# Six weight blocks with stored low parts, and a reordered end, in a one-core hybrid decoder step

## The chip, the cores and the metric

The kernel runs on one core of a Trainium2 chip. The time is device microseconds of one execution; the figure compared is the median over runs. A core has TensorE (PE, matmul), VectorE (DVE), ScalarE (ACT), GpSimd (POOL) and SyncE (SP), which here only issues DMAs; 16 DMA engines carry the transfers that SP and POOL issue.

## The reference, cut to what matters

One step of a two-layer decoder over 1024 prompt tokens and 8 decode tokens, model width 2048, all in f32. Layer 0 is a pooling mixer, layer 1 attention with a window of 128. Both have an input projection to 4096 channels, a gate, an output projection and a LayerNorm over the residual. The change lies in the second layer's output projection and the norm behind it:

```python
    y = (o * jax.nn.silu(gate)) @ w_out
    return layer_norm(ALPHA * x + y, g_ln, b_ln)
```

with

```python
    mu = jnp.mean(xf, axis=-1, keepdims=True)
    var = jnp.mean(jnp.square(xf - mu), axis=-1, keepdims=True)
    return ((xf - mu) * lax.rsqrt(var + LN_EPS) * g + b)
```

## The kernel before

**Two halves, ten phases.** The 1032 tokens are two halves of 512 and 520. `PHASES` runs the projections of the halves in turn; the last two are `bo`, the second layer's output projection, for half 0 and then half 1. Activations stand transposed, 128 channels on the partitions and tokens along the row.

**A product in three.** An f32 product is made of rounded f32r parts: a block of weights (128x1024) is cast to its high part (`cast_to`, ScalarE, L506), the low part is the difference (`prep_to`, VectorE, L521), and TensorE multiplies high by high, high by low and low by high (L687, L688, L689).

**Seven blocks for a pair.** Channels are done in pairs of 128 by a seven-product Strassen form (`seven`). A block is one of the seven, 24 products of 128x128 by half the tokens, named (p, i): pair p of eight, product i of seven. Some blocks are read from the input `wob`, others from sums formed earlier and stored (`swob`). `begin`, ahead of every block, keeps the stream running: it requests weights up to seven blocks ahead (`load_to`, SP's queue), casts up to four and subtracts up to three ahead. After a block its bank of sums is taken up by VectorE or ScalarE in the posts; with `split`, as in the last phase, products 5 and 6 are added on VectorE (L639, L658).

**Order.** Instructions of TensorE, VectorE and ScalarE run in the order of the source (`in_order`); SP's and POOL's are placed by a scheduler. Buffers are 54 slots of SBUF; `Mem.full` hands out the one that was released longest ago, and `free(stored=True)` makes a slot that a store still reads count as released later.

**The end of half 1** is written by hand in `phase_end`. Pairs 4 to 7, called w, x, y, z, run in the order `TAIL`, whose last eight blocks are (4, 5), (4, 6), (5, 5), (5, 6), (6, 5), (6, 6), (7, 5), (7, 6). The half's 520 tokens are cut in two: `Bh`, the second 260, is complete after (w, 5), and its LayerNorm (`stats`, then per pair `affine1` on VectorE, L1493 and L1497, and `affine2` on ScalarE, L1504, with a store) runs while TensorE does the last eight blocks. `A`, the first 260, is complete only after (7, 6). `steps` gives what is issued after each block: `rest` adds the residual, `square` squares (L1456), `add` adds a pair into the running sums av and qv (L1459, L1460), `scale` multiplies by the norm's gain (L1516), `spare` copies the last four tokens aside on POOL (L1519), `back` reloads a pair.

After the last block: `sums_a` multiplies the running sums with J, a matrix of 1/2048 (L1552), `sums_z` adds pair z (L1560): this gives mean and mean square. `turn` transposes the scaled pairs into token rows (L1607). `moments` works out the reciprocal root with a Newton step (L1575 to L1587) and splits the row factors into high and low (`back32`, L1572). `last_rows` adds them to the transposed rows as a product (L1615) with tiles of gain and bias, which `rows0`, `rows1` and `rows2` prepare through a small DRAM tile, `gbd` (twelve row loads, L1542). `evict` takes the rows out (VectorE L1627, ScalarE L1629) and stores them (L1631). `last_four` does the four tokens on POOL (L1639 to L1643).

Of the kernel before, what the change touches and what calls it, by code (L numbers as in the profile page):

```python
# [70 lines left out]
)  # L71

LATE = ()
FORM = (0, 1)
X_KEEP = 5
X_AGE = 3
# [23 lines left out]
class Slot:  # L100


    def __init__(self, mem, i, h, a):
        self.mem, self.i, self.h, self.a = mem, i, h, a

    @property
    def r(self):
# [6 lines left out]
        return self.r[:, : k * n].rearrange("p (k n) -> p k n", k=k)  # L114

    def free(self, stored=False):
        self.mem.release(self, 10 if stored else 0)


class View:  # L120
# [64 lines left out]
class Entry:  # L185


    def __init__(self, loads, make, src, after):
        self.loads, self.make, self.src, self.after = loads, make, src, after


class Kern:
    def __init__(self, ctx, tc, io):
        self.tc, self.io = tc, io
        self.nc = tc.nc
        pool = lambda name, **kw: ctx.enter_context(tc.tile_pool(name=name, **kw))
        one = pool("one", bufs=1)
        self.smp = pool("smp", bufs=2)
        dram = pool("dram", bufs=1, space=bass.MemoryType.DRAM)
        self.psd = [pool(f"psd{i}", bufs=1, space=bass.MemoryType.PSUM) for i in range(3)]  # L200
        self.pso = pool("pso", bufs=1, space=bass.MemoryType.PSUM)
        self.four = None
        ctx.callback(self.use_four, None)
        self.prm = one.tile([P, N_PRM], F32, name="prm")
        self.cst = one.tile([P, N_CST], F32, name="cst")
        self.mki = self.cst[:, K_MP : K_MP + P].bitcast(I32)
        self.jr = one.tile([P, P], F32R, name="jr")
        self.nsink = self.prm[:, C_SINK : C_SINK + NH]
        self.area = one.tile([P, 4 * 64 + 16], F32, name="area")
        cut = lambda a, k, n: self.area[:, a : a + k * n].rearrange("p (k n) -> p k n", k=k)  # L210
        self.carry = cut(0, NK, NST)
        self.qd = [cut(64 * i, NDEC, 8) for i in range(2)]
        self.sgd = [cut(64 * i + 128, 8, NDEC) for i in range(2)]
        self.kdec = cut(256, 2, NDEC)
        self.mem = Mem(pool("mem", bufs=1), NSLOT)
        self.n = 0
        self.i = self.e = self.lastO = self.turns = self.ring = 0
        self.posts, self.events, self.side = [], {}, []
        self.extra, self.on = None, False
        self.fresh = False  # L220
        self.ahead = 7, 4, 3
        dr = lambda n, s: dram.tile(s, F32, tag=n, name=n)
        self.flip = 0
        self.Td, self.act, self.l_sq, self.l_sh = {}, {}, {}, {}
        for c, (_, T) in enumerate(CHUNKS):
            for n, k in (("x", "ai"), ("g", "ao"), ("h", "bi"), ("o", "bo")):
                if (k, c) in STRASSEN:
                    self.Td[n, c] = dr(f"t{n}{c}", [P, 8, 4, T // 2])
            self.act["x", c] = io[f"x{c}"]
            for n in ("g", "h", "o", "p"):  # L230
                self.act[n, c] = dr(f"{n}{c}", [P, NK, T])
        self.gbd = dram.tile([32, 2 * P], F32, tag="gbd", name="gbd")
        self.rows = [dr(f"rows{i}", [2, 32 * TMAX]) for i in range(4)]
        self.turned = 0
        self.ws = {
            n: [dr(f"s{n}{q}", [P, 4, 1024]) for q in range(np_)]
            for n, np_ in (("wia", 16), ("woa", 8), ("wkv", 2), ("wib", 16), ("wob", 8))
        }
# [141 lines left out]
    def build_stream(self):  # L380
        io = self.io
        w = []
        for kind, c, part in PHASES:
# [18 lines left out]
            elif kind == "bi":  # L402
                if part[0] == 0:
                    w += self.next_pairs("wkv", range(2), locked) if seven else pr("wkv", 0) + pr("wkv", 1)
                if seven:
                    for p in range(*part):
                        for q in (p, 8 + p):
                            if c == 1 and p in FORM:
                                f = self.first_pair("wib", q, False)
                                w += [f[i] for i in ORDER7]  # L410
                            else:
                                w += pr("wib", q)
                else:
                    for p in range(*part):
                        q, g = ((self.bare_pair if p in FORM else pr)("wib", q) for q in (p, 8 + p))
                        w += q[:2] + g[:2] + q[2:] + g[2:]
            else:
                name = "woa" if kind == "ao" else "wob"
                if (kind, c, part) != PHASES[-1]:
                    prs = [self.next_pair(name, q) for q in range(8)]  # L420
                    if (kind, c) == ("bo", 0):
                        for q in LATE:
                            prs[q] = self.first_pair(name, q)
                    w += [pr[i] for i in ORDERL for pr in prs[:2]]
                    w += [pr[i] for pr in prs[2:] for i in ORDER7]
                    continue
                w += self.next_pairs(name, range(SPLIT[0]), locked)
                late = {q: self.next_pair(name, q) for q in SPLIT}
                w += [late[q][i] for q, i in TAIL]
        self.stream = w  # L430
        self.loaded = self.made = self.cast = self.prepped = 0
        self.hl, self.late = {}, []

    def sum_gen(self, name):

# [60 lines left out]
    def load_to(self, n):  # L496
        while self.loaded < min(n, len(self.stream)):
            for go in self.stream[self.loaded].loads:
                go()
            self.loaded += 1  # L500

    def cast_to(self, n):
# [13 lines left out]
    def prep_to(self, n):  # L516
        self.cast_to(n)
        while self.prepped < min(n, len(self.stream)):
            s = self.stream[self.prepped]
            hi, lo = self.hl[self.prepped], self.mem.full(1024)  # L520
            self.nc.vector.tensor_sub(lo.r[:, :1024], s.src().a[:, :1024], hi.a[:, :1024])  # L521
            self.hl[self.prepped] = (hi, lo)
            for go in s.after:
                go()
            self.prepped += 1
# [892 lines left out]
    def phase_end(self, c, xs, x_in, pre, acc, gc, bc, out):  # L1418
# [128 lines left out]
        def sums_a():  # L1547

            R[0] = self.psW(), self.psW()
            for ps, a in zip(R[0], (av, qv)):  # L1550
                for j in range(2):
                    nc.tensor.matmul(  # L1552
                        ps[:, :TH], J, a[:, j, A], start=j == 0, stop=False, skip_group_check=True,
                    )

        def sums_z(n):

            w = (tv(z)[:, :, A], qh(z, A))[n]
            for j in range(2):
                nc.tensor.matmul(  # L1560
                    R[0][n][:, :TH], J, w[:, j], start=False, stop=j == 1, skip_group_check=True,
                )

        def moments():

# [13 lines left out]
            nc.vector.scalar_tensor_tensor(v, vb[:, :TH], EPS, qq, op0=ALU.add, op1=ALU.subtract)  # L1579
            affine1a(z, Bh)  # L1580
            nc.scalar.activation(r, v, AF.Abs_reciprocal_sqrt)
            affine2(y, Bh)
            nc.vector.tensor_mul(qq, r, r)
            nc.vector.scalar_tensor_tensor(qq, qq, -0.5, v, op0=ALU.mult, op1=ALU.mult)
            nc.vector.scalar_tensor_tensor(r, qq, 1.5, r, op0=ALU.add, op1=ALU.mult)
            nc.vector.tensor_mul(X[lo], v[lo, A2], r[lo, A2])
            nc.scalar.copy(M[lo], X[lo])  # L1587
            affine1b(z, Bh)
            back32(32)
            back32(96)  # L1590

        def factors():

# [54 lines left out]
        for p in SPLIT:  # L1648
            box, z0, z1 = self.two(T)

            def open_(p=p, box=box, z0=z0):
# [17 lines left out]
            (y, 3): [lambda: rest(x, A), lambda: sh.free()],  # L1669
            (z, 2): [rows0],  # L1670
            (z, 1): [rows1],
            (y, 4): [rows2],
            (z, 3): [lambda: rest(y, Bh), lambda: square(y, Bh), lambda: back(1)],
            (z, 4): [
                lambda: add(y, Bh), lambda: rest(y, A), lambda: back(2), lambda: back(3),
                lambda: spare(0), lambda: scale(0),
            ],
            (w, 6): [lambda: stats(Bh), lambda: spare(1), lambda: scale(1)],
            (x, 5): [lambda: square(w, A), lambda: affine(0, Bh), lambda: spare(2), lambda: scale(2)],
            (x, 6): [lambda: add(w, A), lambda: spare(w), lambda: scale(w)],  # L1680
            (y, 5): [lambda: square(x, A), lambda: affine(w, Bh), lambda: spare(3), lambda: scale(3)],
            (y, 6): [lambda: add(x, A), lambda: affine(1, Bh), lambda: spare(x), lambda: scale(x)],
            (z, 5): [lambda: square(y, A), lambda: affine(2, Bh), lambda: affine1(x, Bh)],
            (z, 6): [
                lambda: square(z, A, 0), lambda: add(y, A), lambda: scale(z, (0,), True), lambda: scale(y),
                lambda: spare(y), lambda: affine1(3, Bh), lambda: affine2(x, Bh),
            ],
        }
        for p, idx in TAIL:
            for go in steps.get((p, idx), []):  # L1690
# [11 lines left out]
        sums_a()  # L1702
        square(z, A, 1)
        affine1(y, Bh)
        scale(z, (1,))
        spare(z)
        sums_z(0)
        sums_z(1)
        X[0, 0], X[0, 1] = self.psD(), self.psD()
        turn(0, 0, 8)  # L1710
        X[0, 2], X[0, 3] = self.psW(), self.psW()
        turn(0, 8, 16)
        moments()
        X[1, 0], X[1, 1] = self.psO(), self.psD()
        turn(1, 0, 8)
        X[1, 2] = self.psW()
        turn(1, 8, 12)
        box["c"] = self.psW()
        factors()
        factors2()  # L1720
        affine2(3, Bh)
        last_rows(0, range(4))
        last_rows(1, range(3))
        evict(0, 0, False)
# [788 lines left out]
```

## Time and profile before

| what | value |
|---|---|
| median of three runs | 2303.64 us |
| lowest and highest | 2302.32 and 2305.52 us |
| the profiled execution | 2304.49 us |
| its span | 2302.7 us |
| PE busy | 2281.3 us (99%) |
| DVE busy | 1907.4 us (83%) |
| ACT busy | 1387.1 us (60%) |
| DMA moved | 654.07 MB, mean 284 GB/s |

The span is from the first to the last instruction. A row of the timeline gives start, length, engine, line, operation, result and operands, and the number merged into it; brackets give the idle time before it and what ended it. Products on TensorE overlap, so a product of 0.28 us is followed by the next after 0.12.

### The profile page before, as it was taken

To read this page: it belongs to the slowest core of one execution; us is meant where nothing else is said; L and a number is where in the kernel's file an instruction comes from. 1 tells how busy PE (TensorE), PEld (TensorE's weight loads), DVE (VectorE), ACT (ScalarE), POOL (GpSimd) and SP (SyncE) were. 2 spreads that over 40 slices of the span, in tenths; PEclk is the share of its full clock that TensorE was granted. 3 is DMA by queue.
4 is the path that set the end of the run, shared out by engine and by line. 5 is a ranking of instruction groups with operands and counts; after the bars stand their busy time and mean duration, and the time that the engine had idled before them with its cause. 6 is when DMAs were issued, how large, how long until landed. Compare 5 with 4: busy or idle time off the path is not lost. (4 is left out here: it accounts for less than half of the span.)

```text
span 2302.7 us, 50591 instructions
## 1 busy us (share of the span) xinstructions
PE 2281.3 (99%) x20353; PEld 2211.2 (96%) x20353; DVE 1907.4 (83%) x2429; ACT 1387.1 (60%) x2551; POOL 218.8 (10%) x399
## 2 busy tenths in 40 slices
PE   9999999999999999999999999999999999999998
PEld 8999999999999999999879999999999999999998
DVE  8888889877878898998868888899876777878997
ACT  5544446544546546655566667785766768656665
POOL 0111110011010010000111111101111010000001
PEclk9999999999999999999999999999999999999999
DMA  7869679988989999999677666777786878699894
GB/s 260 284 246 313 229 253 326 320 302 294 304 316 306 346 352 369 331 379 365 206 268 240 235 223 230 284 271 263 260 274 218 274 258 300 237 327 332 284 330 151
DMA packets 256956, 654.07 MB, mean 284 GB/s; under 512 B 27824, under 2 KB 116944, under 8 KB 256720
## 3 DMA queue, kind: packets, MB, share of 16 engines
q1 hardware_dynamic: 213568, 496.49, 63.7%
q0 software_dynamic: 43152, 154.34, 17.4%
q8 instruction: 159, 2.61, 0.5%
q14 instruction: 77, 0.63, 0.1%
HBM read 473.50 MB, written 177.23 MB: 283 GB/s over the span
## 5 line engine op out<-in xcount | busy, mean ns | idle before, releaser
L687 PE MATMUL pD<-m,m 128*128 128x260 f32 (+1 forms) x5088 | 1442.2, 283 | 3.9 <-ACT pD L626 2.2
L689 PE MATMUL pD<-m,m 128*128 128x260 f32 (+1 forms) x5088 | 1435.3, 282 | 6.1 <-DVE m L521 6.0
L688 PE MATMUL pD<-m,m 128*128 128x260 f32 (+1 forms) x5088 | 1435.0, 282 | 0.0
L687 PEld LDWEIGHTS pD<-m,m 128*128 128x128 f32 x5088 | 959.3, 189 | 13.1 <-issue 7.2
L689 PEld LDWEIGHTS pD<-m,m 128*128 128x128 f32 x5088 | 959.9, 189 | 8.6 <-DVE m L521 8.6
L688 PEld LDWEIGHTS pD<-m,m 128*128 128x128 f32 x5088 | 959.4, 189 | 0.5
L521 DVE TENSOR_TENSOR m<-m,m 128x1024 fp32r<-128x1024 f32 x690 | 832.6, 1217 | 85.7 <-ACT m L506 35.9
L506 ACT CAST m<-m 128x1024 fp32r<-128x1024 f32 x690 | 720.2, 1049 | 231.2 <-DVE m L352 98.8
L352 DVE TENSOR_TENSOR m<-m,m 128x1024 f32<-128x1024 f32 x128 | 156.4, 1222 | 12.2 <-DMA m<-in_wia 6.3
L850 DVE TENSOR_TENSOR m<-m,m 128x1024 fp32r<-128x1024 f32 (+1 forms) x118 | 143.9, 1225 | 3.9 <-ACT m L841 3.0
L841 ACT CAST m<-m 128x1024 fp32r<-128x1024 f32 (+1 forms) x118 | 123.4, 1053 | 3.7 <-DMA m<-in_x 2.4
L648 DVE TENSOR_TENSOR m<-pD,m 128x260 f32<-128x260 f32 (+1 forms) x92 | 39.0, 424 | 100.8 <-ACT pD L647 94.7
L660 ACT COPY m<-pD 128x260 f32<-128x260 f32 (+1 forms) x88 | 32.8, 372 | 122.5 <-PE pD L689 122.1
L1938 ACT ACTIVATE m<-m,sm 128x128 f32<-128x128 f32 x256 | 99.3, 391 | 0.0
L1187 PE MATMUL pD<-m,m 128*128 128x260 f32 (+1 forms) x528 | 91.5, 324 | 0.0
L635 ACT COPY m<-pD 128x260 f32<-128x260 f32 (+1 forms) x92 | 34.4, 373 | 93.1 <-PE pD L689 93.0
L715 PE MATMUL pD<-m,m 128*128 128x512 f32 x224 | 89.1, 398 | 0.0
L717 PE MATMUL pD<-m,m 128*128 128x512 f32 x224 | 88.4, 395 | 0.0
L716 PE MATMUL pD<-m,m 128*128 128x512 f32 x224 | 88.2, 394 | 0.0
L1187 PEld LDWEIGHTS pD<-m,m 128*128 128x128 f32 x528 | 79.4, 188 | 8.2
L632 ACT COPY m<-pD 128x260 f32<-128x260 f32 (+1 forms) x90 | 33.6, 373 | 87.4 <-PE pD L689 86.2
L626 ACT ACTIVATE pD<-pD 128x260 f32<-128x260 f32 (+1 forms) x90 | 33.2, 369 | 83.9 <-PE pD L689 83.4
(258 smaller groups left out, 2142.4 us busy)
## 6 DMA issues: line engine op xcount, KB each, us to landing
m<-in_wib SPq DMA_DIRECT2D x132, 512.0 KB
m<-in_wia SPq DMA_DIRECT2D x128, 512.0 KB
m<-swoa SPq DMA_DIRECT2D x64, 512.0 KB
m<-swob SPq DMA_DIRECT2D x64, 512.0 KB
swia<-m POOLq DMA_DIRECT2D x56, 512.0 KB, 4.7
m<-swia SPq DMA_DIRECT2D x56, 512.0 KB
m<-in_woa SPq DMA_DIRECT2D x48, 512.0 KB
swib<-m POOLq DMA_DIRECT2D x48, 512.0 KB, 4.1
```

What stands on the lines that cost most here:

```text
L352: self.nc.vector.tensor_add(s[out].a[:, :1024], s[x].a[:, :1024], s[y].a[:, :1024])
L506: self.nc.scalar.copy(hi.r[:, :1024], self.stream[self.cast].src().a[:, :1024])
L521: self.nc.vector.tensor_sub(lo.r[:, :1024], s.src().a[:, :1024], hi.a[:, :1024])
L687: nc.tensor.matmul(ps[:, :TH], wh[:, s], h, start=new and k == 0, stop=False, skip_group_check=on)
L688: nc.tensor.matmul(ps[:, :TH], wh[:, s], l, start=False, stop=False, skip_group_check=on)
L689: nc.tensor.matmul(ps[:, :TH], wl[:, s], h, start=False, stop=k == 7, skip_group_check=on)
L715: nc.tensor.matmul(ps[:], wh[:, s], h, start=par == 0 and k == 0, stop=False)
L717: nc.tensor.matmul(ps[:], wl[:, s], h, start=False, stop=par == 1 and k == 7)
L841: self.nc.scalar.copy(h.r[:, :n], s.a[:, :n])
L850: self.nc.vector.tensor_sub(l.r[:, :n], s.a[:, :n], h.a[:, :n])
L1187: nc.tensor.matmul(ps[:, : cs.stop - cs.start], ws[:, s], d[:, cs], start=f0 and k == 0, stop=l0 and k == 3,)
L1938: nc.scalar.activation(x["s3"][:, i, :], x["s3"][:, i, :], AF.Exp, bias=nm[:, i : i + 1], scale=0.125, accum_out=rs[:, i : i + 1],)
```

## The change

- `LOW` names the last six blocks of `TAIL`: (5, 5), (5, 6), (6, 5), (6, 6), (7, 5), (7, 6). In the phase of half 0 their low parts, formed as before, are also stored to DRAM on POOL's queue. In the phase of half 1 these blocks load the low part beside the weights, on SP's queue; the subtraction is left out.
- `rows2` is issued after (w, 6) in place of (y, 4).
- `sums_a` and `sums_z` multiply one column tile each in place of two. A new step `join`, after (z, 6), adds the two halves of av and of qv and the first half of pair z on VectorE, four additions of 128x260.
- `affine1` and `affine2` of half `Bh` are reordered over the blocks: pair 3 moves from the end into the blocks, pair y takes its place after `factors2`. Pair z is scaled inside `moments`, where `affine2(y)` stood, and its two transposes for the first 128 tokens move behind those of the second.
- In `moments`, `affine1b(z)` stands behind the two `back32`.

```diff
+LOW = TAIL[-6:]
...
+        self.low = {k: dr(f"low{k[0]}{k[1]}", [P, 1024]) for k in LOW}
...
+                        for q, i in LOW:
+                            prs[q][i].keep = self.low[q, i]
...
+                for q, i in LOW:
+                    late[q][i].low = self.low[q, i]
                 w += [late[q][i] for q, i in TAIL]
...
                 go()
+            if self.stream[self.loaded].low is not None:
+                lo = self.lows[self.loaded] = self.mem.full(1024)
+                self.nc.sync.dma_start(lo.a[:, :1024], self.stream[self.loaded].low)
...
-            hi, lo = self.hl[self.prepped], self.mem.full(1024)
-            self.nc.vector.tensor_sub(lo.r[:, :1024], s.src().a[:, :1024], hi.a[:, :1024])
+            hi, lo = self.hl[self.prepped], self.lows.pop(self.prepped, None)
+            if lo is None:
+                lo = self.mem.full(1024)
+                self.nc.vector.tensor_sub(lo.r[:, :1024], s.src().a[:, :1024], hi.a[:, :1024])
+            if s.keep is not None:
+                self.nc.gpsimd.dma_start(s.keep, lo.a[:, :1024])
+                lo.stored = True
...
             for ps, a in zip(R[0], (av, qv)):
-                for j in range(2):
-                    nc.tensor.matmul(
-                        ps[:, :TH], J, a[:, j, A], start=j == 0, stop=False, skip_group_check=True,
-                    )
+                nc.tensor.matmul(ps[:, :TH], J, a[:, 0, A], start=True, stop=False, skip_group_check=True)
...
-            for j in range(2):
-                nc.tensor.matmul(
-                    R[0][n][:, :TH], J, w[:, j], start=False, stop=j == 1, skip_group_check=True,
-                )
+            nc.tensor.matmul(R[0][n][:, :TH], J, w[:, 1], start=False, stop=True, skip_group_check=True)
+
+        def join():
+            for a, w in ((av, tv(z)[:, :, A]), (qv, qh(z, A))):
+                nc.vector.tensor_add(a[:, 0, A], a[:, 0, A], a[:, 1, A])
+                nc.vector.tensor_add(a[:, 0, A], a[:, 0, A], w[:, 0])
...
             nc.scalar.activation(r, v, AF.Abs_reciprocal_sqrt)
-            affine2(y, Bh)
+            scale(z, (0, 1), True)
...
             nc.scalar.copy(M[lo], X[lo])
-            affine1b(z, Bh)
             back32(32)
             back32(96)
+            affine1b(z, Bh)
...
-            (y, 4): [rows2],
...
-            (w, 6): [lambda: stats(Bh), lambda: spare(1), lambda: scale(1)],
-            (x, 5): [lambda: square(w, A), lambda: affine(0, Bh), lambda: spare(2), lambda: scale(2)],
-            (x, 6): [lambda: add(w, A), lambda: spare(w), lambda: scale(w)],
-            (y, 5): [lambda: square(x, A), lambda: affine(w, Bh), lambda: spare(3), lambda: scale(3)],
-            (y, 6): [lambda: add(x, A), lambda: affine(1, Bh), lambda: spare(x), lambda: scale(x)],
-            (z, 5): [lambda: square(y, A), lambda: affine(2, Bh), lambda: affine1(x, Bh)],
-            (z, 6): [
-                lambda: square(z, A, 0), lambda: add(y, A), lambda: scale(z, (0,), True), lambda: scale(y),
-                lambda: spare(y), lambda: affine1(3, Bh), lambda: affine2(x, Bh),
+            (w, 6): [lambda: stats(Bh), rows2, lambda: spare(1), lambda: scale(1)],
+            (x, 5): [lambda: square(w, A), lambda: affine(0, Bh), lambda: affine1(w, Bh), lambda: spare(2)],
+            (x, 6): [
+                lambda: add(w, A), lambda: affine2(w, Bh), lambda: affine1(1, Bh), lambda: spare(w), lambda: scale(2),
             ],
+            (y, 5): [
+                lambda: square(x, A), lambda: affine2(1, Bh), lambda: affine1(x, Bh), lambda: spare(3), lambda: scale(3),
+            ],
+            (y, 6): [
+                lambda: add(x, A), lambda: affine2(x, Bh), lambda: affine1(2, Bh), lambda: spare(x), lambda: scale(w),
+            ],
+            (z, 5): [
+                lambda: square(y, A), lambda: affine2(2, Bh), lambda: affine1(3, Bh), lambda: add(y, A),
+                lambda: scale(x), lambda: spare(y),
+            ],
+            (z, 6): [lambda: square(z, A, 0), join, lambda: scale(y), lambda: affine2(3, Bh)],
...
         affine1(y, Bh)
-        scale(z, (1,))
...
-        turn(0, 8, 16)
+        turn(0, 8, 14)
         moments()
         X[1, 0], X[1, 1] = self.psO(), self.psD()
         turn(1, 0, 8)
+        turn(0, 14, 16)
...
-        affine2(3, Bh)
+        affine2(y, Bh)
```

More of the change, by code (lines that the diff above doesn't have):

```diff
@@ L104, in __init__ @@
         self.mem, self.i, self.h, self.a = mem, i, h, a
+        self.stored = False
     @property
@@ L116, in free @@
     def free(self, stored=False):
-        self.mem.release(self, 10 if stored else 0)
+        self.mem.release(self, 10 if stored or self.stored else 0)
 class View:
@@ L189, in __init__ @@
         self.loads, self.make, self.src, self.after = loads, make, src, after
+        self.keep = self.low = None
 class Kern:
@@ L431, in build_stream @@
         self.loaded = self.made = self.cast = self.prepped = 0
-        self.hl, self.late = {}, []
+        self.hl, self.lows, self.late = {}, {}, []
     def sum_gen(self, name):
```

## The prediction

> **What bounds the kernel now.** I read the page first, then the waits of TensorE, then the last 45 us engine by engine in the timeline. Page and waits (waiting engine, line, releaser: us in total, times, longest):
>
> ```profile
> span 2302.7 us, 50591 instructions
> PE 2281.3 (99%) x20353; PEld 2211.2 (96%) x20353; DVE 1907.4 (83%) x2429; ACT 1387.1 (60%) x2551; POOL 218.8 (10%) x399
> PE pD L689 <- DVE m L521: 6.0, 9, 1.4
> ```
>
> TensorE is never short of work for long: 2302.7 - 2281.3 = 21.4 us of idle in all, 6.0 of it waits for the VectorE subtraction that forms the low part of a weight block (L521). Of these, two fall in the last phase:
>
> ```profile
> 2210.49 0.39 PE L689 MATMUL pD<-m,m 128*128 128x260 f32 x1 [0.94 <-DVE m L521]
> 2215.06 0.39 PE L689 MATMUL pD<-m,m 128*128 128x260 f32 x1 [1.43 <-DVE m L521]
> ```
>
> They come some eighteen blocks of 2.88 ahead of the six that the change treats. The rest of the idle is at the end. TensorE there (start, length):
>
> ```profile
> 2284.46 0.28 PE L689 MATMUL pD<-m,m 128*128 128x260 f32 x1
> 2284.58 1.91 PE L1552 MATMUL pD<-m,jr 128*128 128x260 f32 x8
> 2286.33 1.92 PE L1560 MATMUL pD<-m,jr 128*128 128x260 f32 x8
> 2288.08 1.91 PE L1607 MATMUL pD<-cst,m 128*128 128x128 f32 x16
> 2292.84 1.17 PE L1615 MATMUL pD<-m,m 128*128 128x512 f32 x4 [1.32 <-POOL area L1642]
> ```
>
> After the last weight product come the sums over channels (L1552, L1560), the transposes (L1607), then a wait for the row factors before `last_rows` (L1615). The row names POOL as releaser; what L1615 multiplies is written by L1572, which ends at 2292.74. VectorE:
>
> ```profile
> 2273.58 1.22 DVE L521 TENSOR_TENSOR m<-m,m 128x1024 fp32r<-128x1024 f32 x1
> 2274.71 0.69 DVE L1493 TENSOR_TENSOR m<-m,m 128x520 f32<-128x520 f32 x1
> 2284.74 0.69 DVE L1493 TENSOR_TENSOR m<-m,m 128x520 f32<-128x520 f32 x1
> 2286.09 0.42 DVE L658 TENSOR_TENSOR m<-pD,m 128x260 f32<-128x260 f32 x1
> 2286.43 0.69 DVE L1493 TENSOR_TENSOR m<-m,m 128x520 f32<-128x520 f32 x1
> 2287.81 0.43 DVE L1576 TENSOR_TENSOR m<-m 128x260 f32<-128x260 f32 x1
> 2288.34 0.43 DVE L1579 SCALAR_TENSOR_TENSOR m<-pD,m 128x260 f32<-128x260 f32 x1
> 2289.75 0.43 DVE L1584 SCALAR_TENSOR_TENSOR m<-m 128x260 f32<-128x260 f32 x1
> 2290.22 0.43 DVE L1585 SCALAR_TENSOR_TENSOR m<-m,m 128x260 f32<-128x260 f32 x1
> 2290.68 0.42 DVE L1586 TENSOR_TENSOR m<-m,m 64x256 f32<-64x256 f32 x1
> 2291.14 0.70 DVE L1497 TENSOR_TENSOR m<-m,m 128x520 f32<-128x520 f32 x1
> 2291.87 0.87 DVE L1572 TENSOR_TENSOR m<-m,m 32x256 fp32r<-32x256 f32 x2
> 2293.65 3.38 DVE L1627 TENSOR_SCALAR m<-pD,sm 128x512 f32<-128x512 f32 x5 [0.92 <-PE pD L1615]
> ```
>
> The last product ends at 2284.46 + 0.28 = 2284.74, but the addition that takes it (L658) starts at 2286.09: VectorE runs 1.35 us late there. The chain to the end is: sums to about 2288.3, moments L1579 to L1586, the cast on ScalarE, L1572, L1615, the evictions L1627, the stores. ScalarE beside it and on it, and the last full microseconds (after the five busy times: granted clock, DMA share, GB/s):
>
> ```profile
> 2270.45 1.10 ACT L1504 ACTIVATE m<-m,prm 128x260 f32<-128x260 f32 x2 [1.83 <-DVE m L1497]
> 2271.45 0.90 ACT L1516 ACTIVATE m<-m,prm 128x256 f32<-128x256 f32 x2
> 2286.54 0.42 ACT L1456 ACTIVATE m<-m 128x260 f32<-128x260 f32 x1 [0.29 <-DVE m L658]
> 2288.81 0.43 ACT L1581 ACTIVATE m<-m 128x260 f32<-128x260 f32 x1 [0.32 <-DVE m L1579]
> 2291.14 0.40 ACT L1587 CAST m<-m 64x256 fp32r<-64x256 f32 x1 [0.92 <-DVE m L1586]
> 2297.00:2301.00 4.00, 0.00 (x0) 0.00 (x0) 0.04 (x1) 0.00 (x0) 0.00 (x0) 0.77 1.03 404
> ```
>
> The closing 4 us are a pure drain of output at 404 GB/s, which starts when the first evicted rows are stored, so it moves with them.
>
> **Low parts loaded.** Each L521 costs VectorE 2274.71 - 2273.58 = 1.13 us. Of the six, four stand after 2267.5:
>
> ```profile
> L521 DVE TENSOR_TENSOR m<-m,m 128x1024 fp32r<-128x1024 f32 x4 | 4.9, 1215 | 0.0
> L1459 DVE TENSOR_TENSOR m<-m,m 128x520 f32<-128x520 f32 x3 | 2.1, 691 | 0.0
> ```
>
> (groups from 2267 to 2284.7; the third column is the mean in ns.) Removing four frees 4 x 1.13 = 4.5 us just where VectorE is 1.35 us late. The same six pairs of L1493 and L1497 and the same three of L1459 and L1460 stay in the stretch, in another order; four additions of `join` come in. A 128x260 step costs 0.47 when it needs the one before it (2290.22 - 2289.75), and 0.34 when not (2286.43 - 2286.09), so `join` takes 1.4 to 1.9, say 1.7. Work alone would put VectorE at 2286.09 - 4.5 + 1.7 = 2283.3. Since it then waits for TensorE at some blocks, I walked it through: the bank of (z, 5) is complete one block (24 products, 0.12 each, 2.88) ahead of 2284.74, at about 2281.9; its addition and `join` run to 2284.0. That is ahead of the slot 2284.58 at which `sums_a` reads the joined tile. So VectorE is 0.8 us early in place of 1.35 late.
>
> The price is traffic: six stores of 512 KB on POOL's queue in the phase of half 0, and six loads on SP's. Windows (PE, PEld, DVE, ACT, POOL busy, clock, DMA share, GB/s), one landing of a POOL store, and the queue of SP:
>
> ```profile
> 2050.00:2110.00 60.00, 60.00 (x510) 60.00 (x510) 45.87 (x47) 35.88 (x50) 2.38 (x5) 1.00 0.90 315
> 2110.00:2140.00 30.00, 29.88 (x250) 29.67 (x249) 30.00 (x31) 23.18 (x31) 0.54 (x1) 1.00 0.98 357
> 2240.00:2270.00 30.00, 30.00 (x240) 29.54 (x239) 21.64 (x32) 15.20 (x25) 3.42 (x5) 1.00 0.60 202
> p<-m POOLq DMA_DIRECT2D x4, 512.0 KB, 6.8
> 2252.91 7.92 SPq L1542 DMA_DIRECT2D m<-gbd  x12
> 2261.42 0.84 SPq L288 DMA_DIRECT2D m<-in_wob  x2
> ```
>
> Six transfers of 512 KB are 3.1 MB, at 404 GB/s 7.8 us of all engines. For the loads there is room: 40% of 30 us, 12 us, in 2240 to 2270, and the first is needed only at about 2267. For the stores there is 10% of 60 us, 6.0 us, in 2050 to 2110, so up to 7.8 - 6.0 = 1.8 us spill into the full stretch after it. I take 0 for both: TensorE is busy all 60 us there, and weights are requested six to seven blocks (some 18 us) ahead, which hides a push of 1.8. If that cover were gone, up to 7.8 would show; a gain is not in it. Behind a waiting store on POOL's queue stand only later stores; behind a load that waits for a buffer on SP's queue stand the next weights, which have the same 18 us.
>
> **Row loads behind the weights.** The twelve L1542 hold SP's queue 7.92 us, and the last two weight loads go out behind them, at 2261.42. Moved behind (w, 6), they have what follows the weights behind them: the output stores of the other half. `last_rows` reads them at about 2291. Issued from about 2264, twelve take until 2272; 19 us are left. Price 0; bounds -0.1 and 0.3, should a late output store hold a buffer.
>
> **Sums joined.** Four of the eight products with J go; the trace shows two records for each, 2286.33 - 2284.58 = 1.75 for four products. So 2 x 0.875 = 1.75 off TensorE. The `sums_z` products then stand at 2285.45 and 2285.89. Their inputs: L658 at 2284.8 to 2285.2, the square on ScalarE (0.42) to 2285.7. Both are in time. But VectorE takes over as the limit: from L658's start to L1576's start are 1.72 (two L1493/L1497 in between, unchanged), so L1576 starts at 2286.52 and L1579 0.47 later, 2287.0, against 2288.34. Gain 1.34, not 1.75. The bounds: 1.75 if VectorE costs nothing there; 0 if `join` ends late by the 1.35 that L658 is late now.
>
> **Order in the moments.** L1579 to L1586 stays 2.34: L1586 at 2289.34, the cast at 2289.80 to 2290.20. `affine1b` (0.70) no longer stands ahead of L1572. The first of the pair needs no late input and runs under the cast; the second starts at 2290.26, ends at 2290.68; L1615 follows 0.10 later, 2290.78. That is 2292.84 - 2290.78 = 2.06 in all, of which 0.72 is this swap. `affine1b` then ends at about 2291.35, ahead of the first L1627 at 2291.59 (0.81 after L1615, as now). This slack of 0.24 is its cover.
>
> TensorE must have finished the transposes: from 2286.33 it has 28 of 0.109 (1.75 for 16) and two more, done by 2289.7. ScalarE has two `scale(z)` (0.9) after L1581 (ends 2287.9), done at 2288.8, when the moved `turn(0, 14, 16)` comes. After the cast, `affine2(y)` (1.10) holds ScalarE to about 2291.5, and its first eviction comes behind it; the first store also needs VectorE's first L1627, which ends 0.68 (3.38 for five) after 2291.59, at 2292.3, so nothing is lost.
>
> The spread of the other half's norm moves one `affine2` out of the tail into the blocks. ScalarE then has at most a square (0.6), an `affine2` (1.10) and a `scale` (0.90) in a block of 2.88, 2.6; the first two or three have a cast of weights as well and run over a little, which the later ones make up. Price 0, bounds -0.2 and 0.2.
>
> **Sum.** Off 1.34 + 0.72 = 2.06, against this execution's own 2304.49 (span 2302.7 and 1.79 around it): 2302.4. It lies 0.85 above the median 2303.64 of runs from 2302.32 to 2305.52; against the median the forecast is **2301.6**.
>
> A rule that bears on the swap: POOL's copies wait for VectorE.
>
> ```profile
> 2267.86 1.22 DVE L521 TENSOR_TENSOR m<-m,m 128x1024 fp32r<-128x1024 f32 x1
> 2268.00 1.12 POOL L1519 COPY area<-m 128x8 f32<-128x8 f32 x1 [11.04 <-DVE m L658]
> 2291.34 0.66 POOL L1641 TENSOR_TENSOR area<-area,prm 128x64 f32<-128x64 f32 x1
> ```
>
> The copy of 8 columns ends with L521, at 2269.1. The Trainium skill, "SBUF — State Buffer", section "Who interferes with whom", has VectorE with two SBUF inputs and a reading GpSimd lock each other out, whoever starts first; the trace agrees for POOL's side. The other side would be: `last_four` on POOL gets in between the two L1572, now one after the other, and the second waits up to one POOL step, 0.66.
>
> **Rivals.**
> - *Join late.* If VectorE isn't early, the additions stand on the path and only the swap is left, with 0 to 0.6 of the rest: 2303.64 - 0.9 = 2302.7. For it: VectorE is 83% busy and late now. Against: 4.5 us are freed.
> - *POOL in between.* 2.06 - 0.66 = 1.4 off: 2302.2. Against: L1497 ran its usual 0.70 beside L1641.
> - *Upstream stalls go.* Stores that hold their buffers longer change which buffer a later load takes; the two waits of 0.94 and 1.43 could fall away: 2301.6 - 2.4 = 2299.2, a little less with luck elsewhere. Against: nothing of the change takes work from VectorE there.
> - *Stores in the way (slower).* The six stores push the weight loads of the change from half 0 to half 1, where the engines are 0.98 busy. From a delay beyond 2.06 shown by TensorE the kernel is slower: with 2.6 (the last two stores, (7, 5) and (7, 6), 1.05 MB at 404, which fall next to that stretch) 2304.2; with all 7.8, 2309.4. For it: TensorE already loses 0.12 in 2110 to 2140. Against: the requests are far ahead.
> - *It does nothing.* If the low loads landed late, blocks would wait for DMA as they now wait for L521; 12 us of free share speak against it. It is counted with the last.
>
> **How the numbers follow.** Forecast 0.50 (own range 2300.3 to 2303.2: 0.4 either way from the steps, the rest the spread of runs), join late 0.14, POOL 0.06, stalls go 0.15, stores in the way 0.15. A measurement can tell 0.2%, 4.6 us, from no change: faster means under 2299.0, slower over 2308.2. About half of "stalls go" lies under 2299.0: faster 0.08. Of "stores", under half reaches 2308.2: slower 0.06. Within 0.2%: 0.86. The first three cases hold 0.70; with half of each of the other two, 2298.9 to 2305.4 holds 0.8 and a little more.
>
> **What would show it.** L658 of the last block within 0.1 us of the product's end; four records each at L1552 and L1560; the first L1615 6.0 us after the last weight product's end (now 8.1); no L521 after 2267; the drain shifted as a whole. Wrong if the last weight product itself ends at another time than 2284.7 by more than 1 us (upstream), if new waits of TensorE for DMA appear between 2100 and 2140 or after 2260, or if L1627 starts behind `affine1b`.

## The result, and the profile after

The changed kernel takes 2301.2 us (median of 22 runs, 2298.8 to 2303.4), the one before 2305.3 in as many runs beside it (2302.3 to 2307.3): a ratio of 0.9983, interval 0.9977 to 0.9989. That is 3.9 us off, 2.5 to 5.3. The forecast, 2301.6, is 0.4 above the median. Yet it had 2.06 us of gain, taken from 2303.64, and the figure of before turned out 1.7 higher and the gain about twice as large. The time was hit; the sum was not. The medians of experiments 1 and 6 leave out one run each, of 2444.1 and 10950.9 us, in which the granted clock was 0.85 and 0.19.

The changed kernel's lines stand some eleven to sixteen further down: L1615 is L1630 now, L1552 and L1560 are L1567 and L1572, L658 is L674, L1579 is L1594, L1586 is L1601, L1572 of before is L1587, L1627 is L1642, L1497 is L1513, L506 is L517, L521 is L534. The page and TensorE's timeline at the end:

```profile
span 2301.3 us, 50608 instructions
PE 2280.0 (99%) x20345; PEld 2209.3 (96%) x20345; DVE 1902.7 (83%) x2427; ACT 1386.7 (60%) x2551; POOL 220.6 (10%) x405
```

```profile
2284.72 0.28 PE L705 MATMUL pD<-m,m 128*128 128x260 f32 x1
2284.84 1.04 PE L1567 MATMUL pD<-m,jr 128*128 128x260 f32 x4
2285.72 1.04 PE L1572 MATMUL pD<-m,jr 128*128 128x260 f32 x4
2286.59 1.69 PE L1622 MATMUL pD<-cst,m 128*128 128x128 f32 x14
2291.06 1.16 PE L1630 MATMUL pD<-m,m 128*128 128x512 f32 x4 [0.96 <-DVE m L1587]
```

The last weight product ends at 2285.00. The sums have four records each and come without a gap, and the first product with the row factors starts 6.06 us after that end, 8.10 before. VectorE in the same place:

```profile
2285.04 0.43 DVE L674 TENSOR_TENSOR m<-pD,m 128x260 f32<-128x260 f32 x1 [0.72 <-PE pD L705]
2286.76 0.43 DVE L1591 TENSOR_TENSOR m<-m 128x260 f32<-128x260 f32 x1
2287.30 0.43 DVE L1594 SCALAR_TENSOR_TENSOR m<-pD,m 128x260 f32<-128x260 f32 x1
2289.64 0.42 DVE L1601 TENSOR_TENSOR m<-m,m 64x256 f32<-64x256 f32 x1
2290.09 0.87 DVE L1587 TENSOR_TENSOR m<-m,m 32x256 fp32r<-32x256 f32 x2
2290.99 0.70 DVE L1513 TENSOR_TENSOR m<-m,m 128x520 f32<-128x520 f32 x1
2291.88 3.38 DVE L1642 TENSOR_SCALAR m<-pD,sm 128x512 f32<-128x512 f32 x5 [0.19 <-ACT m L1520]
```

L674 waits 0.72 for TensorE and takes the bank 0.04 after the product ends; it was 1.35 late before. L1594 stands 2.30 after that end, 3.60 before. `affine1b` (L1513) is behind L1587 and delays no eviction: the first L1642 starts 0.82 after L1630, 0.81 before.

Upstream two things differ. The windows (share and GB/s are the last two numbers; TensorE's busy time is the second) of before, of the changed kernel, and the waits of TensorE for other engines in the changed kernel from 1960 to 2290:

```profile
2200.00:2220.00 20.00, 17.62 (x145) 17.20 (x143) 16.46 (x15) 11.45 (x18) 0.53 (x1) 1.00 1.01 391
```

```profile
2200.00:2220.00 20.00, 20.00 (x169) 20.00 (x168) 19.42 (x18) 11.14 (x19) 0.54 (x1) 1.00 1.02 396
2110.00:2140.00 30.00, 28.31 (x235) 27.91 (x234) 30.00 (x30) 21.33 (x29) 1.06 (x2) 1.00 1.04 393
```

```profile
PE pD L703 <- ACT m L657: 1.1, 1, 1.1
PE pD L703 <- ACT pD L642: 0.6, 1, 0.6
```

The two waits for the low part at 2209 to 2215 are gone: 2.4 us. In 2110 to 2140, where TensorE was busy 29.88 of 30 before, it now loses 1.7, waiting for ScalarE, which waits for weights. Both lie ahead of the six last blocks, and the sum had nothing for either.

**Comparing executions.** The first changed instruction comes just after 2060, yet the POOL store of a pair at about 2060, which every kernel issues, starts anywhere from 2058.8 to 2063.6 in the profiles of this case:

```profile
2060.11 0.53 POOL L1392 DMA_DIRECT2D p<-m  x1 [9.85 <-ACT m L506]
```

```profile
2061.48 0.53 POOL L1408 DMA_DIRECT2D p<-m  x1 [9.85 <-ACT m L517]
```

So up to 4.8 us between two executions lie in the part that all kernels share. I therefore count from this store on: (a) to the end of the last weight product, (b) from there to the first product with the row factors, (c) from that to the end of the span. "Late release" in the table is the line `lo.stored = True`: the buffers of the six low parts count as released ten releases later.

| kernel | (a) | (b) | (c) | sum |
|---|---|---|---|---|
| before | 224.63 | 8.10 | 9.86 | 242.59 |
| the change | 223.52 | 6.06 | 10.24 | 239.82 |
| the change, profiled again | 222.83 | 6.05 | 10.20 | 239.08 |
| end only (1) | 225.94 | 8.78 | 10.09 | 244.81 |
| low parts only (2) | 223.75 | 8.10 | 10.18 | 242.03 |
| swap only (3) | 224.54 | 7.37 | 9.91 | 241.82 |
| late release only (4) | 221.84 | 8.10 | 9.88 | 239.82 |
| stores meant late (5) | 223.47 | 6.05 | 10.18 | 239.70 |
| the same, small store on POOL (6) | 222.80 | 6.05 | 10.07 | 238.92 |
| four loaded (7) | 221.80 | 6.45 | 10.33 | 238.58 |
| no late release (9) | 226.83 | 6.06 | 10.22 | 243.11 |
| late release and swap (10) | 221.83 | 7.38 | 9.90 | 239.11 |
| four loaded, small store on POOL (11) | 221.79 | 6.45 | 10.21 | 238.45 |

### The profile page after: what moved, and what is told of

It is laid out like the page before. It is cut to its first block, busy times and chain, and to the rows that moved or that the text cites. A ratio compares the mean times of both kernels' runs of the same rounds, so it can differ in the third digit from the quotient of the medians.

```text
span 2301.3 us, 50608 instructions
## 1 busy us (share of the span) xinstructions
PE 2280.0 (99%) x20345; PEld 2209.3 (96%) x20345; DVE 1902.7 (83%) x2427; ACT 1386.7 (60%) x2551; POOL 220.6 (10%) x405
## 4 chain that ended last, share of the span: by engine, by line
PE 87%; DVE 6%; DMA 4%; issue 2%; ACT 1%; SPq 1%; DVEq 0%; ACTq 0%
PE pD L703 24%; PE pD L705 24%; PE pD L704 24%; PE pD L1203 3%; PE pO L2000 2%; DVE m L534 2%; PE pD L731 2%; PE pD L733 2%; PE pD L732 2%; PE pS L1922 2%; PE pS L1975 1%; DVE m L866 1%; DMA m<-swob 1%; DVE m L356 1%; DMA m<-in_x 1%
## 5 line engine op out<-in xcount | busy, mean ns | idle before, releaser
L534 DVE TENSOR_TENSOR m<-m,m 128x1024 fp32r<-128x1024 f32 x684 | 825.5, 1218 | 83.6 <-ACT m L517 37.0
L517 ACT CAST m<-m 128x1024 fp32r<-128x1024 f32 x690 | 720.2, 1049 | 247.7 <-DVE m L356 99.4
L676 ACT COPY m<-pD 128x260 f32<-128x260 f32 (+1 forms) x88 | 32.8, 372 | 120.9 <-PE pD L705 120.6
L1958 ACT ACTIVATE m<-m,sm 128x128 f32<-128x128 f32 x256 | 99.3, 390 | 0.0
L1971 ACT ACTIVATE m<-m,sm 128x128 f32<-128x128 f32 x256 | 81.8, 392 | 2.4 <-DVE sm L1966 2.4
```

What stands on the lines that cost most here:

```text
L517: self.nc.scalar.copy(hi.r[:, :1024], self.stream[self.cast].src().a[:, :1024])
```

## The experiments

Theory: the end gives 2.06 us by its steps, and the rest of the gain is the order of the buffers, which the late release of the six low parts changes. Rivals: all of it comes from the end; or from the relief of VectorE; or the upstream waits are an accident of one execution.

**1. The reordered end without stored low parts.** Against the changed kernel:

```diff
-LOW = TAIL[-6:]
+LOW = ()
```

> The whole change but the low parts: LOW is empty, so the six blocks form their low parts on VectorE as before, and the end keeps join, the order of the norm and the swap in moments. By my steps VectorE then has the four L521 (4.5 us) and join (1.7) in the last stretch, L658 starts some 1.7 us later than before, the moments too, and the swap gives back 0.72: about 1 us slower than before, 0 to 2. If the gain of 4.1 us (2305.3 to 2301.2) came from the reordered end by itself, this kernel would be 3 to 4 us faster than before. If it came from upstream, by the changed buffers, this one would show none of it.

Measured: 2306.3 against 2304.7, ratio 1.0007 (0.9998 to 1.0016). TensorE:

```profile
2286.95 0.71 PE L1567 MATMUL pD<-m,jr 128*128 128x260 f32 x2 [2.01 <-DVE m L1577]
2293.71 1.17 PE L1630 MATMUL pD<-m,m 128*128 128x512 f32 x4 [0.96 <-DVE m L1587]
```

The sums wait 2.0 us for `join` (L1577), and the stretch (b) is 8.78, 0.7 longer than before and 2.7 longer than in the change. The end by itself is no gain; it needs VectorE relieved of the L521 there (two of the four are nearly enough, experiment 7). The stretch (a) is 1.3 longer than before, and that has another cause. TensorE waits 2.2 us for a low part near 2210, once in place of the two waits of 2.4 together, and after it runs at half the clock (granted clock, third from the end):

```profile
2211.00:2214.00 3.00, 3.00 (x16) 3.00 (x15) 3.00 (x4) 1.03 (x2) 0.00 (x0) 0.50 0.97 356
```

A product follows each 0.22 us there in place of 0.12. Before, the clock was 1.00 in the same stretch. It lies some 40 us ahead of the reordered end, so I don't count these 1.3 us as a cost of that; whether other executions of this kernel have them isn't known.

**2. Low parts stored and loaded, the end as before.** Against the kernel before, in part:

```diff
+LOW = TAIL[-6:]
...
+            if self.stream[self.loaded].low is not None:
...
+            if s.keep is not None:
+                self.nc.gpsimd.dma_start(s.keep, lo.a[:, :1024])
+                lo.stored = True
```

> The kernel before with the low parts of the last six blocks stored and loaded, and nothing else. By my steps VectorE is on time at L658 (within 0.1 us of the last product's end, 1.35 late before), but TensorE still makes eight products with J, so that L1579 of before starts where it did, 3.6 us after the last product, and the end gains nothing (0 to 0.2). What this kernel gains beyond that is upstream: 2 us if the two waits of TensorE for L521 at 2209 to 2215 vanish with the changed order of buffers, 0 if they were an accident of one execution, a loss of up to 1.7 if the stores delay the weights at 2110 to 2140.

Measured: 2303.3, ratio 0.9995 (0.9986 to 1.0004). Windows:

```profile
2110.00:2140.00 30.00, 28.34 (x233) 27.73 (x232) 29.89 (x30) 21.11 (x28) 1.06 (x2) 1.00 1.04 383
2200.00:2220.00 20.00, 20.00 (x169) 20.00 (x169) 19.91 (x20) 13.59 (x21) 0.53 (x1) 1.00 1.02 405
```

Both upstream effects come with the low parts alone: the waits at 2200 are gone, 1.7 us are lost at 2110. (b) is 8.10, as before: with L674 0.25 after the last product and not 1.35, nothing is gained while TensorE makes eight sums.

**3. The swap in `moments` alone.** Against the kernel before:

```diff
-            affine1b(z, Bh)
             back32(32)
             back32(96)
+            affine1b(z, Bh)
```

> The kernel before with affine1b moved behind the two back32, and nothing else. My step: 0.72 us off, the first product with the row factors 7.4 us after the last weight product instead of 8.1. Rival: 0, if the final stores, at 404 GB/s, are limited by their bytes and not by their start, or if POOL gets in between the two back32 (0.66 back).

Measured: 2304.05 against 2304.7, ratio 0.9999 (0.9990 to 1.0008): too small for the times. In the trace (b) is 7.37, 0.73 shorter than before, the step as worked out, and (c) is 9.91, so it isn't given back.

**4. The late release alone.** Against the kernel before, in part; the first line is in `free`, which the change has too:

```diff
+        self.mem.release(self, 10 if stored or self.stored else 0)
...
+            if s.keep is not None:
+                lo.stored = True
```

> The kernel before, in which only the six low-part buffers of half 0 count as released ten releases later, as they do in the change; nothing is stored or loaded more. This gives the buffers of the last phase the order that they have in the changed kernel. If the two waits for L521 at 2209 to 2215 hang on which buffer follows which, they vanish here and the kernel is about 2 us faster than before; if they hang on something else, the waits stay and the time is the same within 1 us.

Measured: 2301.9 against 2304.7, ratio 0.9991 (0.9982 to 1.0000); the interval just reaches no change, so the trace has to decide. No instruction is added or moved in the source; what changes is which buffer is handed out next. The window, and the waits of SP's queue from 2185 to 2222 in this kernel:

```profile
2200.00:2220.00 20.00, 20.00 (x169) 20.00 (x168) 19.62 (x20) 13.41 (x21) 0.53 (x1) 1.00 1.02 401
```

```profile
SPq L1343 <- DMA p<-m: 9.0, 1, 9.0
```

and before, with VectorE's wait in the same place:

```profile
SPq L288 <- DMA p<-m: 9.5, 1, 9.5
DVE m L1442 <- DMA m<-h: 3.4, 1, 3.4
```

SP waits some 9 us for a buffer that a POOL store still reads in both. Before, a weight load (L288) is the one that waits; with the late release it is the load of a pair of h (L1343, L1331 of before). The first issues behind that wait, before and then in 4:

```profile
2193.93 0.32 SPq L288 DMA_DIRECT2D m<-swob  x1
2197.87 0.42 SPq L1331 DMA_DIRECT2D m<-h  x1
```

```profile
2193.54 0.32 SPq L1343 DMA_DIRECT2D m<-h  x1
```

So the load of h goes out 4.6 us earlier, counted from the store at 2060 (2.4 in the change). VectorE's wait of 3.4 for h (L1442, which ended at 2206.92 before) doesn't occur, the low parts behind it on VectorE are in time, and TensorE loses nothing. Sum 239.82, 2.8 less than before.

**5 and 6. The last two stores put off; the small store on POOL's queue.** The low parts of (7, 5) and (7, 6) keep their buffers, and their stores stand eighteen blocks later in the source; 6 also issues `y1c`, the small store of the last four tokens, on POOL's queue. Against the changed kernel, in part:

```diff
+                if s.hold:
+                    lo.held = True
+                    self.at(s.hold, lambda s=s, lo=lo: self.let_go(s.keep, lo))
...
-            nc.sync.dma_start(io["y1c"], f3)
+            nc.gpsimd.dma_start(io["y1c"], f3)
```

> The changed kernel, in which the low parts of (7, 5) and (7, 6) keep their buffers and are stored some eighteen blocks (50 us) later than now, past the stretch 2110 to 2140 in which the DMA engines are full; all else is the change. If these two stores make TensorE lose 1.7 us there (28.3 us busy of 30, against 29.8 to 29.9 where nothing is stored), that loss is gone and the kernel is 1.5 us faster than the changed one. Rivals: the four earlier stores push the loads as well, and half of the loss or more stays; or the two buffers that are held change the order of buffers, and the waits of 2.4 us at 2200 to 2220 are back: then 1 us slower than the changed one.

> As the one with the two late stores, and the small store of the last four tokens is issued on POOL's queue, not on SP's, where it now stands between the second and the third of the four large stores and holds the queue 0.6 us. The stretch from the first product with the row factors to the end of the span is 10.2 us in the changed kernel and 9.9 where that store goes ahead of the large ones; if its place makes the difference, 9.9 here, 0.3 off. If the drain is limited by bytes alone, 10.2 stays.

Measured: 2301.0, ratio 0.9985 (0.9976 to 0.9994), and 2301.3, ratio 0.9987 (0.9978 to 0.9996). The edit did not do what it was for. POOL's timeline of 5 has the last two stores where they were:

```profile
2103.85 0.53 POOL L553 DMA_DIRECT2D low<-m  x1 [1.24 <-DVE m L538]
2112.98 0.53 POOL L553 DMA_DIRECT2D low<-m  x1 [8.60 <-DVE m L538]
```

against 2103.13 and 2112.27 in the change: POOL's queue is not in the order of the source. The loss at 2110 to 2140 stays (1.7, and 1.1 in 6). So 5 says nothing of the stores. In 6, (c) is 10.07 against 10.18: the place of the small store costs about 0.1, not 0.3.

**7. Four low parts loaded, two formed.** Against the changed kernel, in part:

```diff
+LOAD = LOW[:4]
...
-                for q, i in LOW:
+                for q, i in LOAD:
                     late[q][i].low = self.low[q, i]
```

> The changed kernel with the low parts of only the first four of the six blocks stored and loaded; (7, 5) and (7, 6) are formed on VectorE as before, and all six buffers keep their late release. Two L521 (2.3 us) come back onto VectorE in the last stretch, which has 0.7 to 0.8 us to spare: L658 of the last block about 1.5 us late, and the end 1.5 us longer than in the change. Upstream, the loss at 2110 to 2140 is gone if the last two stores made it (1.5 us), or half there if all six share it. In sum the same as the change within 1 us, by other waits. If instead the reading of VectorE's slack is wrong and the relief has room, L658 is on time and the kernel 1.5 us faster than the change.

Measured: 2300.9 beside 2300.8 for the change (8); ratios 0.9984 and 0.9985. The last two stores are gone, and with them the loss:

```profile
2110.00:2140.00 30.00, 29.80 (x250) 29.58 (x249) 30.00 (x30) 23.07 (x33) 0.53 (x1) 1.00 0.98 359
```

So the loss of 1.1 to 1.7 hangs on the stores of (7, 5) and (7, 6), 1 MB into a stretch whose engines are full. Whether leaving out any other two would have done as much wasn't tried. The two L521 that come back cost less than I had: (b) 6.45, 0.4 longer and not 1.5. L658 of the last block (L676 in this kernel) is 0.4 us late (2283.24, the product ends at 2282.82).

**8. The change once more.**

> The changed kernel once more, as the yardstick for its neighbours on this chip. By the steps so far: 2.3 us for the waits that the order of buffers takes away, 1.5 back for the stores, 1.7 to 2.1 for the end, 2.5 to 2.9 in all; measured at first were 4.1 (2.5 to 5.3 by the interval). The profile should show again no wait of TensorE at 2200 to 2220, 1.5 to 1.7 us lost at 2110 to 2140, and 6.1 us from the last weight product to the first with the row factors.

Measured: 2300.8 against 2304.7, ratio 0.9985 (0.9976 to 0.9994). The profile has 20.00 of 20 in 2200 to 2220, 28.91 of 30 in 2110 to 2140, and 6.05: as expected, with 1.1 for 1.5 to 1.7.

**9. The change without the late release.** Against the changed kernel:

```diff
-                lo.stored = True
```

> The changed kernel, in which the six stored low-part buffers count as released at once, like all others, and not ten releases later; stores, loads and the end are the change. If the later release takes away the waits at 2200 to 2220 by the order of buffers that it gives, that order is the one of before here, the waits of 2.3 us come back, and from the store of a pair at about 2060 to the last weight product it takes 225 to 226 us (222.8 to 223.5 in the change, 224.6 before): 2 us slower than the change. Rival: the loads of low parts and the traffic shift things by themselves, the waits stay away, and the time is that of the change.

Measured: 2304.9 against 2304.75, ratio 1.0004 (0.9995 to 1.0013). The whole gain is gone. The window and the waits of SP and of VectorE there:

```profile
2200.00:2220.00 20.00, 17.14 (x141) 16.72 (x140) 15.99 (x16) 10.60 (x17) 0.53 (x1) 1.00 0.98 367
```

```profile
SPq L292 <- DMA p<-m: 9.0, 1, 9.0
DVE m L1457 <- DMA m<-h: 3.7, 1, 3.7
```

The picture of before: the weight load waits for the store again, VectorE waits for h, and TensorE loses 2.9. The losses at 2110 stay too, so that the 1.7 us of the end are used up. Experiments 4 and 9 settle the rival of an accident, and the other profiles agree: in the four kernels without the late release (before, 1, 3, 9) TensorE is busy 17.1 to 17.8 of the 20 us, in the nine profiles with it all 20.

**10. Late release and swap, with nothing stored.** Experiments 3 and 4 together.

> The kernel before with the late release of the six buffers and affine1b behind the two back32; no low part is stored or loaded, no join, the order of the norm as before. From the store of a pair at about 2060 to the end of the span it took 242.6 us before, 239.8 with the late release alone, and the swap takes 0.7 off: 239.1, against 239.8 and 239.1 in two executions of the change. So the same time as the change within 1 us, 3.5 us faster than before. Rival: if the relief of VectorE is what counts, it is 2 us slower than the change.

Measured: 2301.2 against 2304.75, ratio 0.9989 (0.9980 to 0.9997); sum 239.11, as worked out. One attribute and one moved line reach the time of the change within what can be measured, without 6 MB of traffic and without `join`. So the rival that the relief of VectorE is what counts falls too.

**11. Four low parts loaded, the small store on POOL's queue.**

> The kernel with four low parts loaded (and six late releases), whose end keeps join, swap and order, and with the small store of the last four tokens on POOL's queue. 238.6 from 2060 to the end without the last edit, 238.4 with it, against 239.1 to 239.8 in the change: 0.7 to 1.3 us faster than the change and about 4 faster than before, if upstream stays free of waits. Rival: other waits come instead, and it is the same as the change.

Measured: 2300.95, ratio 0.9984 (0.9975 to 0.9993). The trace has 238.45, as worked out, 0.6 to 1.4 under the change, but the times can't tell it from the change. It is the shortest of all by the trace, and no more is shown.

## Why the prediction was right or wrong

**The time** was right by luck, because two misses cancelled: the median of before stood on three runs and lay 1.7 us under that of 22, and the gain had parts that the sum set to 0. Of the signs that the prediction named, those of the end came (L658 0.04 after the product, four records each, 6.06 us, the last L521 at 2256.0). Two signs of being wrong came too: new waits between 2110 and 2140, behind late weights, and an upstream that moved. The last weight product ends at 2285.00, close to the 2284.7 named, but only because this execution stood 1.4 us later at 2060 than the one before; from there on, (a) is 1.1 to 1.8 shorter.

**What bounds the kernel now.** The prediction put all idle time of TensorE but the 6.0 of L521 at the end. Of these 15.4 us, 8.7 lie after 2290 (4.04 busy of 12.70); the rest is spread over the kernel.

**Low parts loaded, VectorE.** Right in direction: 0.8 early was forecast, and it waits 0.72 at the last block. Experiment 1 confirms the dependence, and 7 that the relief of two would nearly do; the slack was larger than the walk showed, since two subtractions (2.3 us) cost 0.4.

**Sums joined.** Right: VectorE is the limit after them, L1594 at 2.30 after the last product against 2.26 worked out; gain 1.30 against 1.34.

**Order in the moments.** Right: 0.73 in experiment 3 against 0.72. POOL did not get in between: the two L1587 take 0.42 each and follow without a gap. In all, (b) lost 2.04 of the 2.06 forecast.

**The drain "moves with them".** This step failed by its size: (c) grew from 9.86 to 10.2, so 0.34 to 0.38 of the 2.06 were lost. About 0.1 is the small store's place (6, 11). The rest isn't settled. One candidate is that the output of pair y goes out 0.8 us after the first product with the row factors, where that of pair 3 went out at 0.06, so that its bytes fall into the drain. Experiment 2 speaks against it as the main part: pair 3 goes out 0.04 after that product there, the small store stands in its new place, and (c) is 10.18 already.

**Stores: "I take 0".** Wrong, inside its own bounds: 1.1 to 1.7. The 1.8 us that the prediction had spill into the full stretch came close to this; what failed is the cover. The requests ahead did not hide the spill, because ScalarE casts in order and waited for the late weights (ScalarE's waits for weights, 2105 to 2140, before and after):

```profile
ACT m L506 <- DMA m<-swob: 2.3, 3, 1.6
ACT m L506 <- DMA m<-in_wob: 0.7, 2, 0.5
```

```profile
ACT m L517 <- DMA m<-in_wob: 4.9, 3, 2.8
ACT m L517 <- DMA m<-swob: 4.3, 4, 2.7
```

From 3.0 to 9.2 us, and behind a waiting cast stand the copies of sums (L657) that TensorE needs. The slower rival named this place and these two stores and had 2.6 for them; it just didn't decide.

**Rival "upstream stalls go".** It happened, with 2.4 in the profile of the change and 2.8 in (a) of experiment 4. I gave it 0.15 because nothing takes work from VectorE there; the reason against was true and beside the point, since a buffer's order needs no work. My forecast treated the late release as bookkeeping. It is the largest single term: without it there is no gain (9). That the new order of buffers helps was luck as well: nobody chose it for this.

The account: 2.4 to 2.8 for the buffers, less 1.1 to 1.7 for the stores, 1.7 for the end, 2.8 and 3.5 by the two profiles, 3.9 (2.5 to 5.3) by the times.

## What to carry to other kernels

A "stored" mark that only delays the reuse of a buffer can be worth more than the work it was added for: where an allocator hands out the oldest buffer, one changed time of release can move waits some 100 us further on, for better or worse, so test the mark alone. A kernel that is bound on one engine gains where that engine waits; list those waits first and ask of each part of the change, its bookkeeping too, whether it touches them. Count from a mark that both kernels have just ahead of the first difference, or the part that they share drowns a gain of 0.1%.

## What the runs showed of the hardware

Of six stores of 512 KB, the four issued from 2064 to 2089, where the DMA share was 0.90 before, cost TensorE nothing that shows (60.00 busy of 60 from 2050 to 2110, and 29.80 of 30 behind it in 7). With the two at 2103 and 2112, next to a share of 0.98, TensorE lost 1.1 to 1.7 us; 1.05 MB at 404 GB/s are 2.6 us of the engines.

After one wait of 2.2 us TensorE's granted clock was 0.50 for some 3 us (experiment 1); after the two waits of 0.94 and 1.43 of the kernel before it stayed at 1.00. One profile shows this, and no rule follows from it.

POOL's steps end behind VectorE's, one by one. The additions and products of the last four tokens in the changed kernel:

```profile
2289.75 0.47 POOL L1655 TENSOR_TENSOR area<-area,m 128x64 f32<-128x64 f32 x1 [2.40 <-DVE m L1600]
2290.29 0.38 POOL L1656 TENSOR_TENSOR area<-area,prm 128x64 f32<-128x64 f32 x1
2290.74 0.37 POOL L1657 TENSOR_TENSOR area<-area,prm 128x64 f32<-128x64 f32 x1
```

They end at 2290.22, 2290.67 and 2291.11, each 0.15 to 0.17 after the VectorE step that they overlap (L1601 ends at 2290.06, the two L1587 at 2290.50 and 2290.96). The Trainium skill, "SBUF — State Buffer", section "Who interferes with whom", has the two engines exclude each other when both read SBUF and VectorE has two inputs; the trace agrees for POOL, and shows no VectorE step that was longer for it. In the kernel before, the middle one of these three (L1641) overlapped the longer step `affine1b` and took 0.66 in place of 0.38, while `affine1b` took 0.70 there as in its other places (L1497, 0.699 to 0.702).
